# The first head's probabilities of an eight-head attention turned by VectorE through DRAM, and its weighed sum put behind the second head's gate

## The chip, the cores and the metric

The kernel runs on one core of one Trainium2 chip. The metric is the device time of one execution in microseconds (us); the median of three runs stands for the kernel. Engines are named as the profile names them: PE is TensorE's matmul, PEld its weight load, DVE is VectorE, ACT is ScalarE, POOL is GpSimd, SP is SyncE, which here only issues DMAs.

## The reference

One block of a hybrid model on 512 tokens and 16 meta tokens (528 rows): a feed-forward stage, a retention, an attention over chosen keys, and a second feed-forward stage. The change touches the attention: eight heads of 128, with rotary positions, a softmax over the admitted keys, the weighed sum of the values, and beside it the gates, sigmoids of further projections of the same input `u`.

```python
aq = rope(aq.reshape(B, T, ATT_HEADS, ATT_DH), pos)
ak = rope(ak.reshape(B, T, ATT_HEADS, ATT_DH), pos)
...
ya = dsa_attention(aq, ak, av, iq, ik, iw, k_top).reshape(B, T, ATT_W) @ w_att_out
merged = jax.nn.sigmoid(g_ret) * yr + jax.nn.sigmoid(g_att) * ya
...
# in dsa_attention, per head:
s = jnp.einsum(q, k) * scale          # masked to the admitted keys
p = jax.nn.softmax(s)
out = p[..., :N_META] @ v_meta + p[..., N_META:] @ v_sel
```

(The lines behind the comment are shortened: the reference gathers the chosen keys, the kernel masks the others with a bias.)

## The kernel before

All products are of fp32 accuracy: each operand is split into a high and a low half in a rounded format, and each product is the sum of three matmuls (high by high, high by low, low by high). A split is one copy on ACT (the high half) and one subtraction on DVE (the low half); both are recorded at lines 117 and 118, in `split`.

A projection (queries, keys or a gate) is 8 steps of three matmuls on a weight of 1024 by 128. The weight comes by a DMA on SP's queue into one of two `raw` buffers (L133) and is split into one of three pairs of buffers, `whi` and `wlo`. So a weight's DMA can only be issued once the low half of the weight two before it is subtracted, and a weight's split can only begin once PE has ended the projection three before it.

In the attention stage PE does, head after head: the scores of head h (15 matmuls, `score`), the queries of head h+1 (`psaq`, 24), the keys of head h+1 (`psak`, 48 of 264 columns), the weighed sum of head h-1 (`psao`, 12 and a tail for the meta keys), and a gate (`psgate` or `psga`, 24). Softmax and the rotary step run on DVE, ACT and POOL behind it. The order on each engine is the order in which a scheduler of the language put the instructions when the kernel was built; it holds at run time: each engine, and each queue, takes its instructions in that order and waits where one isn't ready. Tile numbers such as `whi_9979` are the program's own.

The weighed sum wants the probabilities with keys on the partitions, so they are transposed. In the kernel before there are two ways. Heads 1 to 7: `turn` transposes 32 by 32 blocks on DVE into `cross` (L2084), four POOL DMAs write that to DRAM (`pd`, L2088), `turned` reads it back in ten SP DMAs into `land0` to `land3` (L2096, L2100, L2103), one for each 128 keys, and `turned_parts` splits each piece into `pth` and `ptl`. Head 0: `transpose_p` does 14 transposes on PE (L2132, L2134) into PSUM, and the pieces are split from there.

The values of heads 0 to 3 and of heads 4 to 7 are split in two steps, the second behind the sums of the first head and partly behind the scores of the second (`late_v`).

Of the kernel before, what the change touches and what calls it, by code (L numbers as in the profile page):

```python
# [18 lines left out]
P = 128  # L19
# [62 lines left out]
def kernel(ctx: ExitStack, tc: tile.TileContext, x, meta, g1, wg1, wu1, wd1, gm,  # L82
# [77 lines left out]
    class Cols:  # L160


        def __init__(self, src, c0, n, nk=KD, step=2):
            self.src, self.c0, self.n, self.nk, self.step = src, c0, n, nk, step
            self.at, self.raw = 0, None
# [4 lines left out]

        def next(self):
            return split_w(self.next_raw())
# [1258 lines left out]
    def split_values(raw, parts, apart=False):  # L1431
# [5 lines left out]
        late = lambda: nc.vector.tensor_tensor(lo, src, hi.bitcast(F32), ALU.subtract)  # L1437
        if apart:
            return late, split_values_of(parts)
        late()  # L1440
# [557 lines left out]
    with pool("ao") as ao:  # L1998
        vo = [ao.tile([P, AH, S], F32R, tag=f"vo{i}", name="vo") for i in range(2)]
        ao_parts = [(vo[0][:, c, :], vo[1][:, c, :]) for c in range(AH)]  # L2000
        with pool("at") as at:
# [21 lines left out]
            def proj_q(w=None):  # L2023
                w = w or cq.next()
# [10 lines left out]
            def proj_k():  # L2035
                w = ck.next()
                parts, ps = halves(mm_tile("psak"))
                mm3(parts, w, xs, KD)
                return rope_k(ps)

            def rope_k(ps, eng=nc.gpsimd):
# [37 lines left out]

            def turn(h):  # L2080
# [46 lines left out]
            def transpose_p():  # L2127
                parts = []
                for kb in range(4):
                    ps = sm_tile("psPT")  # L2130
                    for j in range(max(kb - 1, 0), 4):
                        nc.tensor.transpose(ps[:, j * P : (j + 1) * P], prob[j][:, kb * P : (kb + 1) * P], ident)  # L2132
                    if kb == 3:
                        nc.tensor.transpose(ps[:NM, 0:P], prob[3][:, 4 * P : T], ident)  # L2134
                    n = S - KQ[kb]
                    ph, pl = part_tiles(kb, n)
                    if kb == 3:
                        split_rows(ps[:NM, P - NM : P], tp["p"][:, :NM], "hlh")
                    split(ps[:, KQ[kb] :], ph, pl)
                    parts.append((ph, pl))  # L2140
                return parts
# [873 lines left out]
```

## Time and profile before

| what | number |
|---|---|
| runs | 1474.12, 1473.36, 1473.56 us; median 1473.56 |
| the profiled execution | 1473.46 us, of which the span of the instructions is 1471.7 us |
| PE busy | 1463.0 us, 99% of the span |
| DVE, ACT, POOL busy | 1136.4 us (77%), 737.1 us (50%), 252.7 us (17%) |
| chain that ended last | 95% of it on PE |

Times in rows are microseconds from the start of the span; 1.8 us of the profiled execution lie outside it. The attention stage that the change touches runs from about 877 to 1070 us. "x13" in a row says that it stands for 13 instructions, and an arrow gives out<-in.

### The profile page before, as it was taken

The numbers are of one execution on the slowest core, as the hardware profiler recorded it, in microseconds if no ns is written. First come the engines' busy times: TensorE is split into PE (matmuls) and PEld (weight loads), VectorE is DVE, ScalarE is ACT, GpSimd is POOL, SyncE is SP. The second block draws the span as 40 slices with busy tenths as digits, with TensorE's granted clock in tenths as the row PEclk, the third lists the DMA queues.
The fourth block names the chain that finished last, engine by engine and source line by source line (L and its number), as shares of the span: only waits on it lengthen the run. The fifth ranks groups of instructions, "written<-read, shape, count | busy, mean of one in ns | idle before, by whom it ended". The sixth has DMA issues, their size and how long they took to land.

```text
span 1471.7 us, 22839 instructions
## 1 busy us (share of the span) xinstructions
PE 1463.0 (99%) x8773; PEld 1299.4 (88%) x8773; DVE 1136.4 (77%) x1761; ACT 737.1 (50%) x1065; POOL 252.7 (17%) x354
## 2 busy tenths in 40 slices
PE   9999999999999999999999999999999999999998
PEld 8999999999988888989898888899888888888886
DVE  5997586686786876687979788778567788888887
ACT  6655264364354445443333428667534645555454
POOL 2001010012311113111111142332101301101100
PEclk9999999999999999999999999999999999999999
DMA  5266476567957839476767664676847347757652
GB/s 176 74 179 177 140 189 166 149 164 209 302 138 246 257 94 310 118 207 161 198 167 194 157 157 114 162 183 172 224 157 257 123 164 268 248 186 271 216 192 94
DMA packets 215502, 270.74 MB, mean 184 GB/s; under 512 B 38368, under 2 KB 137464, under 8 KB 214752
## 3 DMA queue, kind: packets, MB, share of 16 engines
q1 hardware_dynamic: 187104, 204.30, 43.7%
q0 software_dynamic: 25616, 60.23, 18.2%
q10 hardware_dynamic: 2672, 4.74, 1.0%
q8 instruction: 69, 1.13, 0.3%
q14 instruction: 41, 0.34, 0.1%
HBM read 238.01 MB, written 81.54 MB: 217 GB/s over the span
## 4 chain that ended last, share of the span: by engine, by line
PE 95%; DVE 2%; ACT 1%; issue 1%; DMA 0%; POOL 0%; DVEq 0%; ACTq 0%
PE psd L157 9%; PE psqX L157 7%; PE psqX L2539 7%; PE psrg L157 6%; PE psro L157 6%; PE psd L2512 5%; PE psvX L1249 4%; PE psqY L2539 4%; PE psqY L157 4%; PE psrk L157 3%; PE psrq L157 3%; PE psga L157 3%; PE psat L157 3%; PE psmo L157 3%; PE psak L157 3%; PE psaq L157 3%
## 5 line engine op out<-in xcount | busy, mean ns | idle before, releaser
L378 ACT ACTIVATE whi<-raw 128x1024 fp32r<-128x1024 f32 (+2 forms) x165 | 157.3, 956 | 116.9 <-PE psd L157 32.9
L379 DVE TENSOR_TENSOR wlo<-raw,whi 128x1024 fp32r<-128x1024 f32 (+2 forms) x165 | 185.2, 1125 | 22.7 <-ACT whi L378 22.6
L378 ACT ACTIVATE whi<-w 128x1024 fp32r<-128x1024 f32 x58 | 61.3, 1058 | 58.0 <-PE psd L2512 17.2
L379 DVE TENSOR_TENSOR wlo<-w,whi 128x1024 fp32r<-128x1024 f32 x58 | 70.3, 1216 | 22.4 <-ACT whi L378 22.3
L157 PE MATMUL psro<-vo,whi 128*128 128x512 f32 x256 | 78.9, 389 | 0.0
L157 PE MATMUL psd<-hl,whi 128*128 128x264 f32 x352 | 71.4, 284 | 0.0
L157 PE MATMUL psd<-hh,wlo 128*128 128x264 f32 x352 | 70.8, 283 | 0.0
L157 PE MATMUL psd<-hh,whi 128*128 128x264 f32 x352 | 70.6, 282 | 0.0
L118 DVE TENSOR_TENSOR wlo<-raw,whi 128x1024 fp32r<-128x1024 f32 (+1 forms) x43 | 53.9, 1254 | 14.1 <-ACT whi L117 13.8
L157 PE MATMUL psqX<-th,whi 128*128 128x264 f32 x216 | 61.1, 283 | 0.0
L157 PE MATMUL psqX<-tl,whi 128*128 128x264 f32 x216 | 61.1, 283 | 0.0
L157 PE MATMUL psqX<-th,wlo 128*128 128x264 f32 x216 | 61.1, 283 | 0.0
L2418 POOL DMA_DIRECT2D hts<-cross x36 | 23.3, 652 | 208.2 <-DVE cross L2414 207.9
L117 ACT ACTIVATE whi<-raw 128x1024 fp32r<-128x1024 f32 (+1 forms) x43 | 44.2, 1034 | 27.1 <-PE psga L157 10.9
L157 PEld LDWEIGHTS psro<-vo,whi 128*128 128x128 f32 x256 | 48.0, 188 | 10.1
L157 PEld LDWEIGHTS psd<-hh,wlo 128*128 128x128 f32 x352 | 54.5, 188 | 0.0
L157 PEld LDWEIGHTS psd<-hh,whi 128*128 128x128 f32 x352 | 54.2, 188 | 0.0
L157 PEld LDWEIGHTS psd<-hl,whi 128*128 128x128 f32 x352 | 53.8, 188 | 0.0
L378 ACT ACTIVATE whi<-wsum 128x1024 fp32r<-128x1024 f32 x36 | 38.1, 1059 | 30.4 <-PE psd L157 14.8
L157 PE MATMUL psrg<-xh,whi 128*128 128x512 f32 x128 | 50.5, 395 | 0.0
L157 PE MATMUL psrg<-xl,whi 128*128 128x512 f32 x128 | 49.9, 390 | 0.0
L157 PE MATMUL psrg<-xh,wlo 128*128 128x512 f32 x128 | 49.9, 390 | 0.0
(640 smaller groups left out, 4812.0 us busy)
## 6 DMA issues: line engine op xcount, KB each, us to landing
raw<-in_w_in_dram SPq DMA_DIRECT2D x18, 1024.0 KB, 5.9
raw<-in_w_in_dram SPq DMA_DIRECT2D x33, 512.0 KB, 4.2
w<-in_w_in_dram SPq DMA_DIRECT2D x24, 512.0 KB, 6.9
raw<-in_ffn_w_up_dram SPq DMA_DIRECT2D x11, 1024.0 KB, 5.8
raw<-in_ffn_w_gate_dram SPq DMA_DIRECT2D x10, 1024.0 KB, 5.4
w<-in_ffn_w_gate_dram SPq DMA_DIRECT2D x20, 512.0 KB, 4.7
raw<-in_ffn_w_down_dram SPq DMA_DIRECT2D x18, 512.0 KB, 6.9
raw<-in_ffn_w_down_dram SPq DMA_DIRECT2D x12, 768.0 KB, 4.9
```

The source lines that it names most:

```text
L117: nc.scalar.activation(hi, src, AF.Copy)
L118: eng.tensor_tensor(lo, src, hi.bitcast(F32), ALU.subtract)
L157: nc.tensor.matmul(o, a[:, k, :], b[:, sl], start=first and k == 0 and i == 0, stop=last and k == nk - 1 and i == 2, skip_group_check=onto)
L378: nc.scalar.activation(hi, src, AF.Copy)
L379: return lambda: nc.vector.tensor_tensor(lo, src, hi.bitcast(F32), ALU.subtract)
L1249: nc.tensor.matmul(d[bank_][t], a, b[:, k, :], start=not onto and j + k + m == 0, stop=j + k == 3 and m == 2, skip_group_check=onto)
L2418: by.dma_start(d.rearrange("(b i) a e -> a i b e", i=32)[a], cross[32 * a : 32 * a + 32].rearrange("p b c t -> p b (c t)"))
L2512: nc.tensor.matmul(ps[:, t], a, b[:, k, :], start=not onto and k + m == 0, stop=k == 1 and m == 2, skip_group_check=onto)
L2539: nc.tensor.matmul(ps[:, t], a, b[:, k, :], start=not onto and j + k + m == 0, stop=j + k == 3 and m == 2, skip_group_check=onto)
```

## The change

It turns head 0's probabilities as those of the other heads are: `turn(0)` stands behind head 1's keys, `turned(0)` behind that, and the 14 transposes on PE and `transpose_p` are gone. The weighed sum of head 0 goes behind the gate of that iteration instead of ahead of it. To make room and time: `cross` exists from the stage's start, in the bytes that later hold the low halves of the second four heads' values; these values are split at h == 2; the rotary product of head 1's keys is done by DVE instead of POOL; the key weight of head 1 is taken between the first head's scores and the gate's weight right behind them (`ahead`); and the small DMA of the meta keys' block goes from `turn` to `turned`.

```diff
+        def ahead(self):
+            self.held = split_w(self.next_raw())
+            self.at -= 1
...
-        vo = [ao.tile([P, AH, S], F32R, tag=f"vo{i}", name="vo") for i in range(2)]
-        ao_parts = [(vo[0][:, c, :], vo[1][:, c, :]) for c in range(AH)]
+        vo = [ao.tile([P, n, S], F32R, tag=f"vo{i}", name="vo") for i, n in enumerate((AH, 4))]
+        cross = ao.tile([P, 16, 4, 32], F32, tag="vo2", name="cross")
+        ao_parts = [(vo[0][:, c, :], vo[1][:, c, :]) for c in range(4)]
...
-            def proj_k():
-                w = ck.next()
+            def proj_k(w, eng=nc.gpsimd):
...
-                nc.gpsimd.dma_start(land[4], crosst[96 : 96 + NM, NM:])
-
-            def turned(h):
+            def turned(h):
+                nc.gpsimd.dma_start(land[4], crosst[96 : 96 + NM, NM:])
...
-                for to_one in [score(j, q, k) for j in (2, 1, 0, 3)]:
+                to_ones = [score(2, q, k)]
+                wk = ck.next()
+                for to_one in to_ones + [score(j, q, k) for j in (1, 0, 3)]:
                     to_one()
-                vs = split_values(raw, [v[:, :4, :] for v in vo])
-                raw = fetch_values(5, vraw())
+                gr.ahead()
             pend = None
             for h in range(AH):
                 more = h + 1 < AH
                 if h == 1:
                     with tc.manual_schedule(engines=BUSY):
-                        to_ones = [score(j, q, k) for j in (2, 1, 0, 3)]
-                        late_v()
-                        for to_one in to_ones:
+                        for to_one in [score(j, q, k) for j in (2, 1, 0, 3)]:
                             to_one()
+                        turn(1)
+                        pend = turned_parts()
                 elif h:
                     scores(q, k)
                 if more:
-                    q, k = proj_q(w if h == 0 else None), proj_k()
+                    if h:
+                        q, k = proj_q(cq.next()), proj_k(ck.next())
+                    else:
+                        q = proj_q(w)
+                        with tc.manual_schedule(engines=BUSY):
+                            k = proj_k(wk, nc.vector)
+                            turn(0)
+                            vs = split_values(raw, [v[:, :4, :] for v in vo])
+                        turned(0)
+                        raw = fetch_values(5, vraw())
...
+                if h == 1:
+                    wide_gate(sm_tile("psga"))
                 if pend is not None:
-                    (weigh_turned, weigh_v)[h == 1](h - 1, pend, vs[h - 1])
-                if h == 0:
-                    with tc.manual_schedule(engines=BUSY):
-                        late_v, more_v = split_values(raw, [v[:, 4:, :] for v in vo], True)
-                        vs += more_v
-                if h == 1:
+                    weigh_turned(h - 1, pend, vs[h - 1])
+                if h == 2:
...
-                    if more:
-                        turn(h)
-                    wide_gate(sm_tile("psga"))
+                    if h > 1:
+                        if more:
+                            turn(h)
+                        wide_gate(sm_tile("psga"))
                     turned(h)
```

How the built order differs is seen at two places. The first is around head 0's weighed sum, whose pieces come on SP's queue and are split on ACT. On SP's queue the first read of a turned head in the kernel before is head 1's:

```order
L133 DMA raw_9983<-in_w_in_dram 128x8x128
L133 DMA raw_10076<-in_w_in_dram 128x8x128
L133 DMA raw_10185<-in_w_in_dram 128x8x128
L2096 DMA land0_9320<-pd_88 128x512
L2100 DMA land1_9321<-pd_88 128x32
```

After the change the first one is head 0's, and these rows end with its last read (`raw_9977` is the weight of the fourth head's keys, `raw_10082` that of the gate behind head 1's sum, `raw_10192` that of the fifth head's queries):

```order
L133 DMA raw_9977<-in_w_in_dram 128x8x128
L133 DMA raw_10082<-in_w_in_dram 128x8x128
L133 DMA raw_10192<-in_w_in_dram 128x8x128
L2107 DMA land0_9321<-pd_88 128x512
L2111 DMA land1_9322<-pd_88 128x32
L2114 DMA land1_9322<-pd_88 128x4x32 x3
L2111 DMA land2_9323<-pd_88 128x32
L2114 DMA land2_9323<-pd_88 128x4x32 x2
L2111 DMA land3_9324<-pd_88 128x32
L2114 DMA land3_9324<-pd_88 128x4x32
```

So head 0's ten reads stand behind the issue of `raw_10192`. On ACT, after the change, head 0's four pieces (`pth_9679` to `pth_9691`) stand like this (`psak_9747` are the third head's keys, `psgate_9814` is the gate now ahead of the sum):

```order
L117 ACTIVATE whi_9979<-raw_9977 128x1024
L1378 ACTIVATE tmp_9797<-psak_9747 64x528
L1379 ACTIVATE tmp_9797<-psak_9747 64x528
L117 ACTIVATE aq_9737<-tmp_9730 128x512
L117 ACTIVATE whi_10084<-raw_10082 128x1024
L117 ACTIVATE pth_9679<-land0_9321 128x512
L117 ACTIVATE ak_9803<-tmp_9796 128x528
L1476 ACT_TABLE_LOAD
L1476 ACTIVATE gate_9839<-psgate_9814 128x512
L117 ACTIVATE pth_9683<-land1_9322 128x416
L117 ACTIVATE pth_9687<-land2_9323 128x288
L117 ACTIVATE pth_9691<-land3_9324 128x160
```

The first piece stands behind the split of a weight two further on, the other three behind the gate's sigmoid. The second place is DVE around head 1's pieces (the low halves `ptl`), while head 2 is being turned into `cross`. In the kernel before:

```order
L2084 STREAM_TRANSPOSE cross_9816<-pj0_9312 128x5x32
L118 TENSOR_TENSOR ptl_9880<-land1_9321,pth_9879 128x416
L2069 TENSOR_SCALAR pj3_9318<-pj3_9318,stat_9935 128x528
L118 TENSOR_TENSOR wlo_10188<-raw_10185,whi_10187 128x1024
L118 TENSOR_TENSOR ptl_9884<-land2_9322,pth_9883 128x288
L1372 TENSOR_TENSOR tmp_9972<-psaq_9947,cos_9306 128x512
L118 TENSOR_TENSOR ptl_9888<-land3_9323,pth_9887 128x160
```

After the change:

```order
L1380 TENSOR_TENSOR tmp_9966<-psaq_9941,cos_9307 128x512
L2096 STREAM_TRANSPOSE cross_10068<-pj2_9317 128x13x32
L118 TENSOR_TENSOR ptl_9870<-land0_9321,pth_9869 128x512
L1382 TENSOR_TENSOR tmp_9966<-tmp_9966,tmp_9967 128x512
L2096 STREAM_TRANSPOSE cross_10068<-pj1_9315 128x9x32
L2096 STREAM_TRANSPOSE cross_10068<-pj0_9313 128x5x32
L118 TENSOR_TENSOR ptl_9874<-land1_9322,pth_9873 128x416
L118 TENSOR_TENSOR aq_9974<-tmp_9966,aq_9973 128x512
L2096 STREAM_TRANSPOSE cross_10068<-pj3_9319 128x16x32
L2097 STREAM_TRANSPOSE crosst_9326<-pj3_9319 128x32
L118 TENSOR_TENSOR wlo_10195<-raw_10192,whi_10194 128x1024
L118 TENSOR_TENSOR ptl_9878<-land2_9323,pth_9877 128x288
```

All of head 1's low halves, four transposes and a weight's low half now stand behind the rotary product of the fourth head's queries (`psaq_9941`), which in the kernel before came behind the third piece.

## Rows read from the trace of the kernel before

**Rows 1.** The page: busy time of the engines, share of the span, instructions.

```profile
PE 1463.0 (99%) x8773; PEld 1299.4 (88%) x8773; DVE 1136.4 (77%) x1761; ACT 737.1 (50%) x1065; POOL 252.7 (17%) x354
```

**Rows 2.** Waits of PE: us in total, times, longest.

```profile
PE psaq L157 <- DVE ptl L118: 0.3, 1, 0.3
```

**Rows 3.** Windows: length; busy PE, PEld, DVE, ACT, POOL; PEclk, DMA share, GB/s.

```profile
877.00:945.00 68.00, 67.72 (x395) 59.73 (x394) 55.20 (x120) 48.12 (x83) 19.31 (x30) 1.00 0.49 134
945.00:1070.00 125.00, 125.00 (x697) 110.09 (x696) 88.33 (x208) 80.77 (x147) 32.26 (x43) 1.00 0.73 194
```

**Rows 4.** Timeline of PE at head 0's transposes: start, duration, engine, line, operation.

```profile
901.70 1.58 PE L2132 MATMUL psPT<-ident,pj 128*128 128x128 f32 x13
903.12 0.27 PE L2134 MATMUL psPT<-ident,pj 128*16 128x128 f32 x1
903.15 0.48 PE L157 MATMUL psgate<-xh,whi 128*128 128x512 f32 x1
```

**Rows 5.** Timeline of PE at head 1's scores.

```profile
908.73 2.15 PE L2058 MATMUL psS<-ak,aq 128*128 128x400 f32 x15
```

**Rows 6.** Timeline of DVE ahead of head 1's scores.

```profile
906.07 1.22 DVE L118 TENSOR_TENSOR vo<-vraw,vo 128x1024 fp32r<-128x1024 f32 x1
907.21 0.70 DVE L118 TENSOR_TENSOR ak<-tmp,ak 128x528 fp32r<-128x528 f32 x1
```

**Rows 7.** The chain that ended last, 900 to 960: start, duration, engine, tile.

```profile
916.88 5.77 PE psak L157 x48
922.65 1.90 PE psao L1624 x12
...
924.61 5.59 PE psgate L157 x24
...
943.44 1.96 PE psao L2123 x12
```

**Rows 8.** Timeline of ACT, 929 to 936.

```profile
930.01 1.06 ACT L117 ACTIVATE whi<-raw 128x1024 fp32r<-128x1024 f32 x1 [1.40 <-PE psgate L157]
931.09 1.28 ACT L1471 ACT_TABLE_LOAD   x1
932.39 0.60 ACT L1471 ACTIVATE gate<-psgate 128x512 f32<-128x512 f32 x1
...
934.93 0.20 ACT L1454 ACTIVATE ptail<-land 16x16 fp32r<-16x16 f32 x1
```

**Rows 9.** The tile land: duration in ns (min/median/max), first and last start, forms.

```profile
L117 ACT ACTIVATE pth<-land x28: 321/490/634, 935.9 to 1067.5; 128x512 fp32r<-128x512 f32 x7, 128x416 fp32r<-128x416 f32 x7, 128x288 fp32r<-128x288 f32 x7, 128x160 fp32r<-128x160 f32 x7
L118 DVE TENSOR_TENSOR ptl<-land,pth x28: 310/571/1684, 936.6 to 1067.9; 128x512 fp32r<-128x512 f32 x7, 128x416 fp32r<-128x416 f32 x7, 128x288 fp32r<-128x288 f32 x7, 128x160 fp32r<-128x160 f32 x7
```

**Rows 10.** Timeline of SP's queue: the first and the last read of head 1.

```profile
930.70 0.34 SPq L2096 DMA_DIRECT2D land<-pd  x1
...
936.10 0.52 SPq L2103 DMA_DIRECT2D land<-pd  x1
```

**Rows 11.** DMA issues, 880 to 960: count, KB each, median us to landing.

```profile
land<-pd SPq DMA_DIRECT2D x11, 64.0 KB, 2.6
land<-pd SPq DMA_DIRECT2D x2, 256.0 KB, 3.4
```

**Rows 12.** The tile cross: DVE's transposes.

```profile
L2084 DVE STREAM_TRANSPOSE cross<-pj x28: 302/546/714, 916.5 to 1047.7; 128x416 f32<-128x416 f32 x7, 128x288 f32<-128x288 f32 x7, 128x160 f32<-128x160 f32 x7, 128x512 f32<-128x512 f32 x7
```

**Rows 13.** The tile psao: DVE's subtraction of 512 columns.

```profile
L118 DVE TENSOR_TENSOR vo<-psao,vo x8: 676/684/693, 927.9 to 1069.7; 128x512 fp32r<-128x512 f32 x8
```

**Rows 14.** Timeline of DVE around head 2's last piece, 950 to 968.

```profile
965.38 0.32 DVE L118 TENSOR_TENSOR ptl<-land,pth 128x160 fp32r<-128x160 f32 x1
965.95 1.22 DVE L118 TENSOR_TENSOR wlo<-raw,whi 128x1024 fp32r<-128x1024 f32 x1 [0.25 <-ACT whi L117]
```

**Rows 15.** Windows behind the last matmul (columns as in rows 3).

```profile
1465.70:1467.00 1.30, 0.00 (x0) 0.00 (x0) 1.18 (x3) 1.17 (x4) 0.00 (x0) 1.00 0.56 217
...
1468.00:1469.00 1.00, 0.00 (x0) 0.00 (x0) 0.00 (x0) 0.00 (x0) 0.00 (x0) 0.50 0.83 327
```

More of the change, by code (lines that the diff above doesn't have):

```diff
@@ L164, in __init__ @@
             self.src, self.c0, self.n, self.nk, self.step = src, c0, n, nk, step
[L165 removed]
+            self.at, self.raw, self.held = 0, None, None
         def next_at(self, i):
             self.at = i
+        def ahead(self):
+            self.held = split_w(self.next_raw())
+            self.at -= 1
         def next(self):
[L172 removed]
+            if self.held is None:
+                return split_w(self.next_raw())
+            w, self.held = self.held, None
+            self.at += 1
+            return w
         def next_raw(self):
@@ L1429, in tails, with split_values @@
         tp.update(v=stacked(p, "vtail", S), p=stacked(p, "ptail", n))
-    def split_values(raw, parts, apart=False):
+    def split_values(raw, parts):
         src, (hi, lo) = raw[:, 2:4], (p[:, 2:4, :] for p in parts)
@@ L1436, in split_values @@
         nc.scalar.activation(hi, src, AF.Copy)
[L1437 to L1440, printed above, removed]
+        nc.vector.tensor_tensor(lo, src, hi.bitcast(F32), ALU.subtract)
         return split_values_of(parts)
@@ L2078, in part_tiles, with empty @@
                 return [at.tile([P, S - Q0[kb]], F32R, tag=f"pt{c}{kb}", name=f"pt{c}")[:, :n] for c in "hl"]
+            def empty(t):
+                for j in range(3):
+                    nc.gpsimd.memset(t[:, 4 * j + 5 :, j, :], 0.0)
+                return t
+            empty(cross)
             def turn(h):
@@ L2125, in weigh_turned @@
                 split(ps, *ao_parts[h])
[L2127 to L2141, printed above, removed]
-            def weigh_v(h, parts, v):
-                ps = mm_tile("psao")[:, :S]
-                weighted(ps, v, parts)
-                split(ps, *ao_parts[h])
             def wide_gate(tile=None):
@@ L2190 @@
                         turn(h)
+                if h == 1:
+                    wide_gate(sm_tile("psga"))
                 if pend is not None:
-                    (weigh_turned, weigh_v)[h == 1](h - 1, pend, vs[h - 1])
-                if h == 0:
-                    with tc.manual_schedule(engines=BUSY):
-                        late_v, more_v = split_values(raw, [v[:, 4:, :] for v in vo], True)
-                        vs += more_v
-                if h == 1:
+                    weigh_turned(h - 1, pend, vs[h - 1])
+                if h == 2:
+                    for r in (0, 2):
+                        nc.scalar.activation(vo[0][:, 4 + r : 6 + r, :], raw[:, r : r + 2], AF.Copy)
+                    vo.append(ao.tile([P, 4, S], F32R, tag="vo2", name="vo"))
+                    more_v = [vo[0][:, 4:, :], vo[2]]
+                    for r in (0, 2):
+                        hi, lo = (p[:, r : r + 2, :] for p in more_v)
+                        nc.vector.tensor_tensor(lo, raw[:, r : r + 2], hi.bitcast(F32), ALU.subtract)
+                    vs += split_values_of(more_v)
+                    ao_parts += [(more_v[0][:, c, :], more_v[1][:, c, :]) for c in range(4)]
                     vrs.close()
                     crp = crs.enter_context(pool("cross", 1, side="right"))
-                    cross = crp.tile([P, 16, 4, 32], F32, tag="cross", name="cross")
-                    for j in range(3):
-                        nc.gpsimd.memset(cross[:, 4 * j + 5 :, j, :], 0.0)
+                    cross = empty(crp.tile([P, 16, 4, 32], F32, tag="cross", name="cross"))
                 if h:
-                    if more:
-                        turn(h)
-                    wide_gate(sm_tile("psga"))
+                    if h > 1:
+                        if more:
+                            turn(h)
+                        wide_gate(sm_tile("psga"))
                     turned(h)
```

8 lines of the change are left out of this document (3 added, 5 removed).

## The prediction

> **What bounds the kernel now.** I read the page first: PE is busy in 99% of the span [rows 1], so a wait of PE costs its own length, and work taken from another engine gains nothing by itself. Then the windows of the stretch that the change touches: 67.72 busy of 68.00 us up to 945, and 125.00 of 125.00 after it, at a granted clock of 1.00 [rows 3]. Then PE's waits, to see what the missing 0.28 is: one wait of the third head's queries for a low half of head 0's probabilities, whose PSUM bank they take [rows 2]. The reader is to see that this stage has nearly no wait to give back. The change can gain by taking matmuls away, and it loses wherever a piece now comes late. So I walked each weighed sum with the new order of the instructions and the durations of the rows. All times are of one profiled execution of 1473.46 us, 0.1 below the median of the three runs; its span is 1471.7, and the sum is made against 1473.46.
>
> **What is saved.** The 14 transposes on PE start at 901.70 and the gate behind them at 903.15 [rows 4]: 1.45 us from start to start, 0.104 each. The wait of 0.28 [rows 2] goes, since that PSUM tile is gone. Head 0's sum, in the wider form of the other heads, takes 1.96 instead of 1.90 [rows 7]. Together -1.67.
>
> The last transpose's own duration is 0.27 [rows 4], but they overlap, and the step from start to start is what PE pays. The Trainium skill, "TensorE: Matmul & The Clock Gate", Part 4: PE-mode transpose, gives about 275 ns for one such transpose inside a kernel. By that, 14 would be worth 3.85 us, and the whole forecast would be 2.4 lower, 1478.8. The row agrees with the 275 ns as a duration, and not as a price in a run of them, so 1.45 stands.
>
> **Wait B: head 1's scores for their keys.** Before, the low half of these keys ends at 907.21 + 0.70 = 907.91 and the scores start at 908.73 [rows 6, 5]: 0.82 to spare. PE now comes 1.45 earlier. If the keys are ready when they were, the scores wait 0.4, as the low half is wanted one product in (2.15 for 15, [rows 5], so 0.14), and 1.45 - 0.82 - 0.14 leaves some 0.4 to 0.5. On DVE a subtraction of values (1.22, [rows 6]) goes out of the way and a weight's low half of the same size comes in, with the rotary product (about 0.7, as a DVE row of 528 columns, [rows 6]). The lower bound is 0, if the removal of all three subtractions ahead of it outweighs that; the upper is 1.6, if one 1.22 is added to the 0.4. I take 0.6, nearer to the case in which things stay.
>
> **Wait C: head 0's sum.** Let E be the end of the third head's key products; before it is 916.88 + 5.77 = 922.65 [rows 7]. Then comes the gate, 5.59, and then the sum, 1.96 [rows 7], which would end at E+7.5 with no wait. Two chains come later than that.
>
> The first is that of SP's queue. The fourth head's key weight takes the third one's buffer, so its high half starts at E; 1.06 on ACT [rows 8], 1.22 on DVE for its low half [rows 6], E+2.3. Only that frees the buffer into which `raw_10192` goes, and the ten reads of head 0 stand behind that issue. With 0.6 for handing on and for issuing the weight the first read goes out at E+2.9. Ten reads take from 930.70 to 936.10 in the row [rows 10], so the last goes out at E+8.3. A read of 64 KB lands in 2.6 (the first, 256 KB, in 3.4) [rows 11]: E+10.9. Then a copy of 0.32 and a subtraction of 0.31, the least of their rows [rows 9], and the last product and the tail, 0.3: the sum ends at E+11.8. That is 4.3 of waiting.
>
> The second is ACT's order. `whi_10084` waits for the end of the gate, as its like before waited 1.40 for one [rows 8]; behind it come the first piece, the keys' high half, the table load, the sigmoid and three pieces. From the gate's end: 1.06 + 0.62 + 0.65 + 1.28 + 0.60 with 0.62 as the middle of the wide pieces of 0.49 to 0.63 and 0.65 as an estimate for 528 columns from the same [rows 8, 9], then 0.54 + 0.45 + 0.32 for the pieces (sum of three within 0.32 to 0.63, [rows 9]) and 0.6 for the last subtraction and product: 6.1, against 2.0 for a sum that doesn't wait. That is 4.1; where the first piece is not yet there or the keys' high half waits for DVE, up to 0.9 more. I take 4.6. Lower bound 3, if reads issue and land faster than in the row; upper 6, if DVE's order adds one more subtraction of 1.22 in front.
>
> What is queued behind: head 2's scores wait on PE itself, the fourth head's queries behind them. POOL has time.
>
> **Wait D: head 1's sum, third piece.** Let Q be the end of the fourth head's query products. Behind Q ACT does a weight's high half 1.06, two meta pieces of 0.2 and two rotary halves of 0.6 as the gate's row [rows 8]: 2.66. Then DVE has, in the new order, the cosine product 0.68, four transposes at 0.546 [rows 12] = 2.18, a narrow one of under 0.2, three low halves of pieces at 0.57 [rows 9] = 1.71, the sum of the rotary step and the queries' low half at 0.68 each [rows 13], and a weight's low half 1.22: 7.3. So the third piece is there at Q+10.0. PE comes to that product after the keys (5.77, [rows 7]) and some two thirds of the sum (1.4): Q+7.2. A wait of 2.8; a DVE instruction starts a little before the one ahead is recorded as ended (906.07 + 1.22 = 907.29 against 907.21, [rows 6]), so I take 2.7, with 1 (half of DVE's rows done before the cosine product's turn) and 3.3 (one more low half of 0.57 ahead) as the bounds. In the kernel before, the same pieces stood ahead of the cosine product and nothing waited.
>
> **Wait E: head 2's sum, last piece.** Before, this low half ends at 965.38 + 0.32 = 965.70, and right behind it comes a weight's low half, 965.95 to 967.17 [rows 14]. PE's need was at about 966.0 (the sum of head 2 starts 20.8 behind that at 943.44, by the step of the two sums in [rows 7], and the last piece is 1.75 into it), so 0.3 was to spare. In the new order the weight's halves stand ahead of that piece: it is ready at 967.17 + 0.32 = 967.5, a wait of 1.5. Bounds 0.5 and 2. From head 3 on, the order around the sums is that of before, and PE runs with no wait again; nothing in that stretch gives time back, as PE had none to give [rows 3].
>
> The rest of the edits costs nothing: the values' second split lies behind heads 2's softmax, on engines busy for 65 to 71% there [rows 3]; the moved DMA of 1 KB stands on POOL, which is 26% busy.
>
> **Sum.** -1.67 + 0.6 + 4.6 + 2.7 + 1.5 = +7.7: 1473.46 + 7.7 = **1481.2**. Its own range is 1478.5 to 1483.5. A measurement of this kernel tells 0.2%, 2.9 us, from no change.
>
> **Rivals.**
> 1. Only B and C are paid. After C, PE is 4.6 later, and DVE and ACT have used that time to come ahead; head 1's and head 2's pieces are then in time. For it: both waits are sums of many short steps with a spread. Against: the late pieces are late against query products of the same head, which are pushed back as well. -1.67 + 0.6 + 4.6 = +3.5: 1477.0.
> 2. Not slower: the reads of head 0 land in time. If the first read goes out about 4.3 earlier than E+2.9, that is ahead of the weight's issue, and the pieces stand ahead of the sigmoid, C is gone, and with C the late start of D and E. For it: the probabilities themselves are in DRAM long before. Against: SP's and ACT's orders. At most -1.67: 1471.8. As that is 0.11%, faster by over 0.2% has hardly a way.
> 3. PE's clock falls in C. In a stretch of 1.30 us with no matmul the granted clock was still 1.00, and a microsecond behind that stretch it was 0.50, 1.2 GHz [rows 15]. If the waits of C brought it down for the scores that follow (2.15, [rows 5]), these would take twice as long: +2.2, 1483.4. Against: products stand between the pieces of C, so no single idle time is as long as that. The Trainium skill, "TensorE: Matmul & The Clock Gate", Part 1, says that the gate has these two levels and follows PE's activity; the rows agree, and no row of this stage shows it below 1.00.
>
> **How the numbers follow.** The forecast 0.55, only B and C 0.20, not slower 0.08, the clock 0.10, and 0.07 for anything else. The range is 1475.5 to 1485.0: the low end takes in nearly all of rival 1 and the sum of the low bounds (-1.67 + 0 + 3 + 1 + 0.5 = +2.8, 1476.3), the high end rival 3 and the sum of the high ones (-1.67 + 1.6 + 6 + 3.3 + 2 = +11.2, 1484.7). Slower by over 0.2% (above 1476.4) has the forecast, the clock, over half of rival 1 and most of the rest: 0.82. Within 0.2% has the other part of rival 1 and rival 2: 0.16. Faster: 0.02.
>
> **What would show it.** In PE's waits after the change: no row with psPT; head 1's scores on their keys for 0.6; head 0's sum on its pieces for 4 to 5 in all, in three or four parts; head 1's on one low half for 2.7; head 2's on one for 1.5; none in heads 3 to 7. SP's timeline shows the first read of head 0 right behind a weight's issue. The prediction is wrong if that read goes out before E, if the gate's end doesn't hold the first piece's copy back, or if the trace shows PE busy through 920 to 950.

## The result, and the profile after

The changed kernel takes 1489.17 us (median of five runs, 1486.99 to 1490.16) against 1473.93 for the kernel before on the same chips: ratio 1.0102, interval 1.0088 to 1.0117, 15.2 us slower. The forecast was slower by 7.7, so the sign and the places were right, and the size was half of the measured one; 1489 lies above the range. The profiled execution took 1490.1, 0.9 above the median, with a span of 1488.3.

PE's waits, on the page's terms the first thing to read (us in total, times, longest):

```profile
PE psao L2134 <- ACT pth L117: 5.2, 3, 3.0
PE psao L2134 <- DVE ptl L118: 4.0, 4, 1.5
...
PE psS L2062 <- DVE ak L118: 0.2, 1, 0.2
```

The wait of the third head's queries [rows 2] is gone, the sums of heads 0 to 2 wait, head 1's scores wait 0.2. These rows make 9.4 us; the loss is 15.2 in the medians and 16.6 in this execution. The windows show what is missing (columns as in rows 3; PEclk is the third number from the end):

```profile
900.00:925.00 25.00, 24.75 (x144) 21.69 (x144) 20.63 (x41) 18.28 (x27) 7.70 (x9) 1.00 0.68 189
925.00:950.00 25.00, 18.88 (x90) 14.95 (x89) 17.01 (x42) 14.01 (x28) 6.16 (x8) 0.80 0.62 141
950.00:975.00 25.00, 23.54 (x132) 20.45 (x131) 20.04 (x46) 15.22 (x28) 6.78 (x12) 0.93 0.57 148
975.00:1000.00 25.00, 23.30 (x130) 20.44 (x129) 17.70 (x42) 14.98 (x28) 5.41 (x7) 0.93 0.57 144
1000.00:1070.00 70.00, 70.00 (x393) 61.93 (x393) 52.60 (x127) 48.67 (x86) 20.73 (x28) 1.00 0.72 189
```

Up to 925 and from 1000 on PE is as full as before [rows 3]. Between, it idles 9.3 us in three windows, and in all three the granted clock is below 1.00. Finer windows of the same kernel:

```profile
926.00:928.00 2.00, 0.25 (x2) 0.00 (x0) 2.00 (x7) 1.58 (x2) 0.00 (x0) 1.00 1.09 338
928.00:930.00 2.00, 0.69 (x1) 0.19 (x1) 2.00 (x3) 1.38 (x3) 1.83 (x3) 0.85 0.98 174
930.00:932.00 2.00, 1.05 (x2) 0.50 (x2) 1.51 (x3) 1.99 (x3) 0.98 (x3) 0.50 1.07 200
...
938.00:940.00 2.00, 2.00 (x11) 1.99 (x10) 0.71 (x3) 1.88 (x2) 0.36 (x1) 0.59 0.62 116
940.00:942.00 2.00, 2.00 (x14) 1.78 (x14) 2.00 (x12) 1.36 (x5) 0.00 (x0) 1.00 0.47 73
...
954.00:956.00 2.00, 0.73 (x7) 0.73 (x7) 2.00 (x5) 0.81 (x2) 0.76 (x2) 1.00 0.01 2
956.00:958.00 2.00, 2.00 (x8) 1.64 (x8) 2.00 (x2) 0.60 (x1) 2.00 (x3) 0.68 0.93 204
958.00:960.00 2.00, 2.00 (x6) 1.52 (x5) 1.57 (x3) 0.39 (x1) 1.63 (x3) 0.50 1.03 333
```

In head 0's sum the clock goes to 0.50 (1.2 GHz) while PE mostly waits, and is back only when head 2's scores are nearly done. At head 1's sum PE does 0.73 in 954 to 956 at 1.00, and it is the gate behind the wait that runs at 0.50, with PE busy all the time. The DMA engines are full here: shares of 1.09, 0.98 and 1.07. Single windows of 2 us reach that in the kernel before too (1.09 in 948 to 950); what is new is that it lasts. In windows of 5 us, first after the change, then before it:

```profile
925.00:930.00 5.00, 1.94 (x7) 0.90 (x5) 5.00 (x9) 2.96 (x5) 2.45 (x4) 0.94 0.95 229
930.00:935.00 5.00, 3.00 (x5) 1.29 (x5) 2.83 (x4) 2.17 (x3) 2.07 (x3) 0.50 1.03 235
```

```profile
925.00:930.00 5.00, 5.00 (x23) 4.13 (x22) 4.00 (x5) 2.01 (x3) 2.99 (x4) 1.00 0.49 115
930.00:935.00 5.00, 5.00 (x29) 4.44 (x29) 3.24 (x13) 4.93 (x7) 1.29 (x1) 1.00 0.80 198
```

The starts of PE's groups in the two timelines, and the difference, tell where each microsecond went:

| start of | before | after | later by |
|---|---|---|---|
| gate behind the second head's keys | 903.15 | 901.37 | -1.78 |
| third head's keys | 916.72 | 914.84 | -1.88 |
| their end, E | 922.49 | 920.61 | -1.88 |
| third head's scores (behind gate and head 0's sum) | 930.04 | 937.91 | +7.87 |
| fourth head's queries | 932.03 | 940.77 | +8.74 |
| head 1's sum | 943.27 | 952.01 | +8.74 |
| gate behind it | 945.30 | 956.00 | +10.70 |
| next scores | 950.84 | 963.18 | +12.34 |
| head 2's sum | 964.08 | 976.42 | +12.34 |
| gate behind it | 966.11 | 980.65 | +14.54 |
| next scores | 971.66 | 987.78 | +16.12 |
| last head's sum | 1066.92 | 1082.88 | +15.96 |

So head 0's sum lost 9.75, the scores behind it 0.87 (slow), head 1's sum 1.96, the gate behind it 1.64 (slow), head 2's sum 2.20, the gate behind it 1.58 (slow); heads 3 to 6 nothing. The last sum lost another 0.8.

How head 0's sum came to end so late stands in the chain that ended last (start, duration, what), read from the wait backwards:

```profile
911.46 8.47 DMA vraw<-vst
...
919.95 1.91 ACT vo L2197 x2
...
921.90 1.07 ACT whi L117
...
922.99 1.24 DVE wlo L118
...
924.25 0.37 SPq L133
...
924.79 0.45 SPq L2107
...
928.40 0.52 SPq L2114
...
928.97 6.50 DMA land<-pd
...
935.57 0.45 ACT pth L117
...
936.06 1.90 PE psao L2134 x6
```

It is the predicted chain, weight's high half, low half, the queue, the reads, the piece, with two transfers in it that are much longer than thought: the load of values (1 MB) took 8.47 (5.0 in the kernel before), so the first read left at E+4.2 instead of E+2.9; and a read of the third piece took 6.5 instead of 2.6 [rows 11]. Beside it, the writes of head 1's turn went out at 928.17 to 930.81 on POOL.

### The profile page after: what moved, and what is told of

It is laid out like the page before. It is cut to its first block, busy times and chain, and to the rows that moved or that the text cites. A ratio compares the mean times of both kernels' runs of the same rounds, so it can differ in the third digit from the quotient of the medians.

```text
span 1488.3 us, 22860 instructions
## 1 busy us (share of the span) xinstructions
PE 1469.8 (99%) x8759; PEld 1301.5 (87%) x8759; DVE 1139.1 (77%) x1767; ACT 737.4 (50%) x1065; POOL 257.0 (17%) x361
## 5 line engine op out<-in xcount | busy, mean ns | idle before, releaser
L157 PEld LDWEIGHTS psro<-vo,whi 128*128 128x128 f32 x256 | 48.0, 188 | 10.2
```

Of the source, the lines that this page charges most:

```text
L157: nc.tensor.matmul(o, a[:, k, :], b[:, sl], start=first and k == 0 and i == 0, stop=last and k == nk - 1 and i == 2, skip_group_check=onto)
```

## The experiments

Every ratio is to the kernel before on the same chip. "Loses" is what a group takes beyond its time in the kernel before, its waits and slow matmuls taken together, in the profiled execution.

**1. Fillers in the waits.** Matmuls that nobody reads keep PE busy while it waits.

```diff
+            FILL = {0: {(0, 0): 13, (0, 1): 6, (1, 0): 2, (1, 1): 5, (2, 0): 8}, 1: {(2, 1): 6}, 2: {(3, 0): 3, (3, 1): 4}}
...
+                        for _ in range(FILL.get(h, {}).get((kb, i), 0)):
+                            nc.tensor.matmul(both[:, S:], vh, xs(0)[0][:, REAL], start=True, stop=True)
```

> The changed kernel, with matmuls that nobody reads put into the waits of the first three weighed sums: 13, 6, 2, 5 and 8 of 512 columns (0.23 us each) ahead of five products of head 0's sum, 6 ahead of one of head 1's, 3 and 4 ahead of two of head 2's. They write into the second, unused bank of the sum's own PSUM tile, so the result is the same. Theory A (each long wait lets PE's clock fall, and the slow matmuls behind it cost as much as a wait): the granted clock stays at 1.00 through 925 to 990, the scores behind head 0's sum take 2.0 instead of 2.86, the gates behind head 1's and head 2's sums 5.55 instead of 7.2 and 7.1, some products of head 0's sum 1.1 less: about 5 us less than the changed kernel, 1484. Theory B (the waits alone make the 15 us, the clock is a side effect that is hidden in them): the same time as the changed kernel, 1487 to 1490, or more by what the fillers overrun.

1484.86 us, ratio 1.0072 (1.0055 to 1.0089): 4.3 less than the changed kernel, for work added.

```profile
925.00:950.00 25.00, 24.52 (x127) 20.22 (x126) 20.13 (x48) 15.19 (x31) 7.55 (x11) 1.00 0.65 154
950.00:975.00 25.00, 25.00 (x153) 22.57 (x152) 19.78 (x45) 14.93 (x27) 7.54 (x10) 1.00 0.62 163
```

The clock stays at 1.00, the scores behind head 0's sum take 2.1, the gates 5.55. The sums still end as late (11.6 behind the gate for head 0, 11.8 in the changed kernel). The clock's part is shown: some 4 of the 15, as the three slow groups behind the sums make in the table above (0.87, 1.64 and 1.58).

**2. Reads of head 0 early on SP's queue; the queue in written order for two iterations.**

```diff
+                    sp.enter_context(tc.manual_schedule(engines={mybir.EngineType.SP}))
...
+                if h in (1, 2):
+                    if h == 2:
+                        ga.ahead()
+                    rq = cq.next_raw()
+                    turned(h - 1)
+                    pend = turned_parts()
...
```

The split of the pieces is written behind the reads with them.

> The changed kernel, with SP's queue in written order for the second and third iteration, so that head 0's ten reads stand ahead of the weight of the fourth head's keys instead of behind the two weights after it; head 1's reads come behind the weights as before. Theory A (head 0's sum waits for reads that leave late and land slowly because they meet the writes of the next head): the first read leaves at about 916 instead of 924.8, the pieces have landed before the gate ends, and head 0's sum waits some 2.5 for ACT's and DVE's order alone, instead of 9.8 from the gate's end; with one fall of the clock less the total is 1479 to 1483. Theory B (the place of the pieces on ACT, behind a weight that waits for the gate's end and behind the sigmoid, sets the wait wherever the reads land): the sum ends still 4 to 6 later than without a wait, and the total stays above 1484.

1488.56 us, ratio 1.0102 (1.0087 to 1.0117). The first read leaves at 920.38, and head 0's sum ends 3.4 earlier behind the gate, with 6.4 of loss instead of 9.8. That is close to theory B (4 to 6, above 1484): DVE's order holds the pieces now. And head 1's sum loses 5.9 instead of 2.0; nothing is left in the total. PE's rows of the two sums:

```profile
928.95 0.50 PE L2135 MATMUL psao<-ptl,vo 128*128 128x512 f32 x1 [1.44 <-DVE ptl L118]
...
932.36 0.72 PE L2135 MATMUL psao<-ptl,vo 128*128 128x416 f32 x1 [1.76 <-DVE ptl L118]
...
955.36 0.61 PE L2135 MATMUL psao<-ptl,vo 128*128 128x288 f32 x1 [3.54 <-DVE ptl L118]
```

**3. Only the gate ahead of the sum, in the kernel before.**

```diff
+                if h == 1:
+                    wide_gate(sm_tile("psga"))
                 if pend is not None:
...
-                    wide_gate(sm_tile("psga"))
+                    if h > 1:
+                        wide_gate(sm_tile("psga"))
```

> The kernel before with one edit: the second head's gate ahead of the first head's weighed sum. The transposes on PE, the values and the rotary product stay as they were. If the order of gate and sum by itself breaks the order on ACT and DVE for the sums of heads 1 and 2 (theory B2), there are waits of 1 to 2 us at these sums, and 1476 to 1480. If only the way through DRAM makes pieces late (theory A), no wait but at most 0.4 us, 1473.5 to 1474.5.

1474.68 us, ratio 1.0007 (0.9997 to 1.0016). The order of gate and sum costs nothing that can be told.

**4. Head 1's turn late,** behind head 0's sum.

```diff
-                        turn(1)
                         pend = turned_parts()
...
+                    if more:
+                        turn(h)
                     if h > 1:
-                        if more:
-                            turn(h)
                         wide_gate(sm_tile("psga"))
```

> The changed kernel with head 1's turn (five transposes on DVE, four writes of 256 KB to DRAM) behind head 0's weighed sum, where those of the later heads stand, instead of ahead of the third head's queries. Theory A's part on the landing (the last reads of head 0 took 6.5 us because they met these writes): the third and fourth pieces land 2.6 to 3.5 after their issue, head 0's sum waits 3 less, and head 1's reads come later instead, so that head 1's sum waits for them: 1486 to 1490 in total, but with the wait moved from head 0's sum to head 1's. Theory C (the weights on the same queue, not the writes, slow the reads): landing stays at 6 us and head 0's sum as it is.

1493.83 us, ratio 1.0130 (1.0113 to 1.0146): worse than expected. Head 0's third piece came 2.1 earlier (its copy started at 933.44), which is the part of head 1's turn in the 6.5; but head 1's sum lost 4.4 and head 2's 4.1.

**5. Head 0 on PE again, the rest of the change kept** (`transpose_p` and `weigh_v` are the functions of the kernel before).

```diff
-                        pend = turned_parts()
...
-                            turn(0)
...
-                        turned(0)
...
-                    weigh_turned(h - 1, pend, vs[h - 1])
+                    (weigh_turned, weigh_v)[h == 1](h - 1, pend, vs[h - 1])
...
                 else:
+                    pend = transpose_p()
                     wide_gate()
```

> The changed kernel with head 0's probabilities transposed on PE again as in the kernel before, so head 0 has neither the turn on DVE nor writes nor reads; everything else of the change stays (the gate ahead of the sum, the values split at the third head, the rotary product of the second head's keys on DVE, the weights taken early). Theory A (the way of head 0 through DRAM makes the waits): no wait at the weighed sums, the clock stays up, and at most a wait of 3 at the third head's scores for their keys, which the order of ACT and DVE now puts late: 1473.5 to 1477.5. Theory D (the other edits, by the order that they give to ACT and DVE, make the sums of heads 1 and 2 late on their own): waits of 1.5 to 2 with a slow gate behind each at these two sums, 1480 to 1484.

1481.85 us, ratio 1.0050 (1.0035 to 1.0065). The time is theory D's, but no sum waits; the place is the one that theory A named, with waits of 3.8 and 0.9 instead of at most 3, and slow matmuls behind them: 7 us are lost there.

```profile
PE psS L2062 <- ACT ak L117: 3.8, 1, 3.8
...
PE psS L2062 <- DVE ak L118: 1.1, 2, 0.9
```

The third head's scores wait for their keys, and run slow behind the wait. On ACT and POOL:

```profile
928.59 1.06 ACT L117 ACTIVATE whi<-raw 128x1024 fp32r<-128x1024 f32 x1 [4.54 <-DMA raw<-in_w_in_dram]
...
932.45 0.64 ACT L117 ACTIVATE ak<-tmp 128x528 fp32r<-128x528 f32 x1
```

```profile
919.58 2.60 POOL L2100 DMA_DIRECT2D pd<-cross  x4 [6.67 <-issue]
922.20 1.31 POOL L1381 TENSOR_TENSOR tmp<-tmp,sin 128x512 f32<-128x512 f32 x1
...
924.12 1.66 POOL L1381 TENSOR_TENSOR tmp<-tmp,sin 128x528 f32<-128x528 f32 x1 [0.62 <-ACT tmp L1379]
```

The four writes of head 1's turn stand in one piece ahead of the rotary products, and the keys (`ak`) stand on ACT behind a weight that lands late: ACT waits 4.54 for it. The second of these orders is what counts, and DVE has it too: its sum of the rotary step comes at 930.82, behind the low half of that weight. POOL's product for the keys had ended at 925.78.

**6. Reads early as in experiment 2, and head 0's sum behind the fourth head's queries.**

```diff
-                        q, k = proj_q(cq.next()), proj_k(ck.next())
+                        q = proj_q(split_w(rq) if rq is not None else cq.next())
+                        if h == 2:
+                            weigh_turned(0, pend, vs[0])
+                        k, rq = proj_k(ck.next()), None
...
-                if pend is not None:
+                if pend is not None and h > 1:
```

> The kernel with the early reads (e2_reads_early) and head 0's weighed sum behind the fourth head's queries instead of behind the second head's gate. Theory A: by then all pieces of head 0 have long come, so there is no wait at its sum; what is late instead are the third head's keys for the scores right behind the gate (2 to 3), and head 1's pieces (4 to 6, as in e2_reads_early): 1480 to 1486. If the order on DVE holds head 0's pieces back wherever the sum stands, its wait of 6 stays and the total is above 1488.

1488.81 us, ratio 1.0095 (1.0078 to 1.0112); the profiled execution was the slowest of its runs (1493.52), so only its order of events is used: head 0's sum had no wait, and the third head's keys and head 1's pieces were late in its place. The total missed the expected range.

**7 and 8. No reads of head 0; no reads of head 1.** The sum goes over what the tiles hold, in experiment 7 and 9 zeros that POOL wrote once.

```diff
             def turned(h):
                 nc.gpsimd.dma_start(land[4], crosst[96 : 96 + NM, NM:])
+                if h == 0:
+                    return
```

In experiment 8 it is `if h == 1`, in 9 `if h < 2`.

> The changed kernel without head 0's ten reads: its pieces are split from a buffer of zeros, so this head's output is left out, and the time is that of the kernel without these transfers. Theory A: the wait at head 0's sum loses what the reads make of it, 3 to 5 of 9.8, and what is left (1 to 3) is the order on DVE, and 2 to 3 of wait at the third head's scores for their keys; heads 1 and 2 keep their waits: 1483 to 1487. Theory B (order on ACT and DVE alone): the sum of head 0 ends as late as before, 1488 to 1490.

> The changed kernel without head 1's ten reads: its pieces are split again from what head 0 left, so this head's output is left out, and the order on ACT and DVE is one in which they don't wait for a transfer. Head 0's sum keeps its 9.8. If head 2's wait follows from head 1's lateness (theory E1), both waits and both slow gates go: 2.0 + 1.6 + 2.2 + 1.6 = 7.4 less than the changed kernel, 1481.8. If head 2's wait has its own cause in the order of its last piece (theory E2), only head 1's part goes: 1485.5.

Without head 0's reads 1490.77 us, ratio 1.0110 (1.0095 to 1.0125), above both theories: head 0's sum loses 0.8 instead of 9.8, but the scores behind it, which wait for their keys, now lose 4.7, and the sums of heads 1 and 2 lose 5.1 and 5.0. Without head 1's reads 1484.35, ratio 1.0067 (1.0052 to 1.0082): head 2's sum takes 2.02 and the gate behind it 5.54, no wait at all. The waits and slow gates of both heads go, as theory E1 says (the total falls by 4.8 instead of its 7.4). So head 2's wait doesn't stand by itself; it comes with head 1's reads.

**9. No reads of either.**

> The changed kernel without the ten reads of head 0 and without those of head 1 (zeros are split and weighed, both heads' outputs are left out). Theory A2 (a late chain: whatever is taken from head 0's sum comes back at the next thing that is late, the third head's keys, and at head 2's sum): waits of 3 to 6 at the third head's scores, some at head 2's sum, 1481 to 1486. Theory A (the reads of both heads make the time): 1473 to 1477.

1486.99 us, ratio 1.0089 (1.0074 to 1.0104). Head 0's sum loses 1.9, the third head's scores 3.8 (3.0 of it waits for their keys), the queries behind them 1.3, head 2's sum 5.9 and the gate behind it 1.1: what was taken from the first place came back at the next. That is theory A2, 1 us above its range.

**10. Values' first split and the load of the others back to their old place.**

```diff
                 gr.ahead()
+                vs = split_values(raw, [v[:, :4, :] for v in vo])
+                raw = fetch_values(5, vraw())
...
                             turn(0)
-                            vs = split_values(raw, [v[:, :4, :] for v in vo])
                         turned(0)
-                        raw = fetch_values(5, vraw())
```

> The changed kernel with the first four heads' values split, and the load of the others' (1 MB) issued, ahead of the second head's queries as in the kernel before, so this load no longer runs beside the writes of head 0 and ahead of the weight of the fourth head's keys. Theory G (the load of 1 MB, which took 8.5 us, holds back the copies of values on ACT, the weight behind them, and with it the reads of head 0): the first read leaves 1.3 earlier after the third head's keys than 4.2, head 0's sum waits 1.3 to 3 less, and the second head's scores wait up to 1 more for their keys: 1485.5 to 1488. Otherwise the time of the changed kernel, 1487 to 1490.

1487.77 us, ratio 1.0097 (1.0082 to 1.0113). The first read left at 924.28, E+2.9, the predicted time; head 0's sum lost 8.1 instead of 9.8. In the total it can't be told from the changed kernel. One thing in this run speaks against a simple rule for the clock. Head 1's sum has the same wait of 1.46, with PE's busy time nearly that of the changed kernel in 954 to 956, and yet the gate behind it runs at full clock (5.55):

```profile
954.00:956.00 2.00, 0.83 (x7) 0.83 (x8) 2.00 (x5) 0.72 (x2) 0.86 (x2) 1.00 0.07 6
956.00:958.00 2.00, 2.00 (x11) 1.66 (x10) 2.00 (x1) 0.60 (x1) 2.00 (x3) 1.00 0.92 237
958.00:960.00 2.00, 2.00 (x10) 1.65 (x10) 1.48 (x3) 0.49 (x1) 1.53 (x3) 1.00 0.96 311
```

**11. Head 0 on PE, and head 1's turn late:** the diffs of experiments 4 and 5 together.

> The changed kernel with head 0's transposes on PE again (e5_pe_again) and head 1's turn, with its four writes, behind head 0's weighed sum, where the kernel before has it, instead of ahead of the third head's queries. e5_pe_again lost 7 us at the third head's scores, which waited for their keys. Theory F (the place of head 1's turn makes these keys late: its four writes go out on POOL in one piece ahead of the rotary products, and ACT's order then has a weight that comes late ahead of the keys): the waits go but for 0.5 to 1, 1473.5 to 1476. Theory G (the load on the DMA engines, by the values' load that now falls into this stretch, makes the weight and so the keys late): the wait stays at 3 or more, 1478 to 1482.

1474.30 us, ratio 1.0007 (0.9997 to 1.0016): as fast as the kernel before. Against experiment 5 only the place of head 1's turn differs in the program, and with it some 7 us go (7.5 between the medians, 6.9 when each is taken against the kernel before). The built order differs by more than the turn. On ACT the keys now stand ahead of the late weight:

```profile
928.36 0.64 ACT L117 ACTIVATE ak<-tmp 128x528 fp32r<-128x528 f32 x1 [2.19 <-DVE tmp L1382]
928.91 1.04 ACT L117 ACTIVATE whi<-raw 128x1024 fp32r<-128x1024 f32 x1
```

On POOL a write, the rotary product of the queries and a write alternate again, but the product of the keys comes no earlier; it ends at 926.61, against 925.78 in experiment 5:

```profile
925.29 1.32 POOL L1381 TENSOR_TENSOR tmp<-tmp,sin 128x528 f32<-128x528 f32 x1 [3.10 <-ACT tmp L1379]
```

So of theory F the order on ACT is borne out, and the four writes ahead of the rotary products are not what made the keys late.

**12. Head 0's sum ahead of the gate again,** the rest as changed.

```diff
-                if h == 1:
-                    wide_gate(sm_tile("psga"))
                 if pend is not None:
                     weigh_turned(h - 1, pend, vs[h - 1])
+                if h == 1:
+                    wide_gate(sm_tile("psga"))
```

> The changed kernel with head 0's weighed sum ahead of the second head's gate, as in the kernel before; head 0 still goes through DRAM. If the gate ahead of the sum covers its own length of the wait (theory A), the sum ends about where it did, some 17 behind the third head's keys, and the gate comes behind it, slow: 5.5 to 7 more, and 1.5 to 3.6 less at the sums of heads 1 and 2 for which PE then comes later: 1490 to 1494. If the supply on ACT, DVE and the queue sets the pace whatever PE does in the meantime (theory A2), the later waits shrink by as much as the first grows: 1487 to 1490.

1488.93 us, ratio 1.0115 (1.0093 to 1.0137). That is theory A2: head 0's sum now loses 14.6 instead of 9.8, the slow group behind it 1.4, and the sums of heads 1 and 2 nothing. The gate ahead of the sum is worth nothing here.

**13 to 15. What head 0's turn costs when nobody needs it.** Into the kernel of experiment 11 comes `turn(0)` alone, then `turned(0)` too, while PE still turns head 0's probabilities itself; and the kernel of experiment 7 gets head 1's turn late (the diff of experiment 4).

```diff
                             k = proj_k(wk, nc.vector)
+                            turn(0)
                             vs = split_values(raw, [v[:, :4, :] for v in vo])
+                        turned(0)
```

> The kernel with PE's transposes for head 0 and head 1's turn late (e15_pe_turn1, 1474.3), with head 0's five transposes on DVE and its four writes of 256 KB added; nobody reads what they write. Theory H (head 0's turn costs by itself, through DVE's time and the DMA engines, before any piece is read): the second head's softmax or the third head's keys come late, waits of 4 to 6 with a slow stretch, 1479 to 1482. Theory I (only the reads and the pieces of head 0 cost): 1474 to 1476.

> The same with head 0's ten reads too, into the buffers that head 1's reads use next; head 0's sum still takes PE's transposes. Theory H: 2 to 5 more than e20_turn0_write, as the reads stand ahead of head 1's on the queue and head 1's sum waits: 1481 to 1487. Theory I: 1477 to 1481 against 1474 to 1476 for e20_turn0_write.

> The changed kernel without head 0's ten reads (zeros are split and weighed, this head's output is left out) and with head 1's turn behind head 0's sum. If two causes are each enough (the reads of head 0, the early turn of head 1), taking both away gives 1475 to 1479. If head 0's turn alone already makes head 1 late (theory H), head 1's sum waits 5 to 7 with slow matmuls behind it, 1484 to 1490.

1481.70 us (ratio 1.0052, 1.0037 to 1.0067), 1484.53 (1.0075, 1.0058 to 1.0092) and 1488.65 (1.0098, 1.0083 to 1.0113). The turn on DVE and its writes cost 7.4 with no reader, the reads 2.8 more. The loss of the first is in several small waits at a clock of 1.00: 1.3 of the third head's queries for DVE, 2.3 of the third head's scores for keys, 1.1 of head 1's sum, 0.6 of head 2's. All three totals lie where theory H puts them. DVE had been full there already; of 5 us, in experiment 11 and then in 13 (the third pair of numbers is DVE):

```profile
910.00:915.00 5.00, 5.00 (x26) 4.23 (x26) 4.97 (x12) 4.44 (x8) 1.30 (x1) 1.00 0.83 272
```

```profile
910.00:915.00 5.00, 3.73 (x21) 3.06 (x20) 4.94 (x9) 3.40 (x5) 3.70 (x5) 1.00 0.73 138
```

PE goes from 5.00 to 3.73 where DVE has no room for the turn.

## Why the prediction was too low

In the profiled execution the loss is 16.6, where 7.7 were forecast. Of the 8.9 between them 5.1 are the size of wait C, the slow matmuls inside it counted in, and 4.1 are slow matmuls behind the three sums, for which the sum had no term; the other differences nearly cancel.

- **What is saved** (-1.67): right. From the second head's keys to the gate the gain grew from 0.33 to 1.78, so the 14 transposes were worth 1.45; at E it was 1.88.
- **Wait B** (+0.6): 0.25.
- **Wait C** (+4.6): the place and both chains were right, the size was not: 9.75, above the bound of 6. Two durations were taken from a quieter stretch. The step "a read of 64 KB lands in 2.6" measured 6.5 for the third piece, and the load of values, which the change moves into this stretch, 8.47; experiments 4 and 10 give 2.1 and some 1.7 back by taking head 1's writes and this load away; the rest of the 5.1 has no run of its own. I had counted head 0's reads, and not the two moves that put a megabyte each into the same microseconds.
- **The rivals, clock** (+2.2 in one place, chance 0.10): the granted clock fell three times, and filling the waits gave 4.3 back (experiment 1). "No single idle time is as long as that" (1.30) was wrong for C, where PE waited 3.0 in one piece; and it was asked of C alone, although the forecast had single waits of 2.7 and 1.5 at D and E. So the premise that a wait of PE costs its own length is a step that failed: at head 1's sum 1.46 of waiting were followed by a gate 1.64 longer. It doesn't fail each time: behind the same wait in experiment 10 the gate lost nothing, and what decides it no run here shows.
- **Waits D and E** (+2.7, +1.5): 1.96 and 2.20. In D it was the predicted piece that waited (PE 955.27, 1.46 for DVE). In E it was the last piece, as forecast. But that this is a wait of its own, by the order of that piece, is not borne out: in experiments 2, 8 and 12 the same sum ran without a wait.
- **"The rest of the edits costs nothing":** for what that sentence names it held, as experiment 11 keeps all of the change but head 0's way through DRAM and the place of head 1's turn, and takes 1474.30. What it left out failed in kind. Head 1's turn ahead of the third head's queries costs some 7, by the order that ACT and DVE get with it (experiment 5 against 11), and head 0's turn 7.4 before any piece of it is read (experiment 13 against 11). I had costed neither at the place where it displaces other work, only the waits for their pieces.

The theory that I held after the result, that late reads make the wait, fell too: head 0's reads early (experiment 2), without them (7) and without those of both heads (9), the total stayed within 2.2 us; only without head 1's alone (8) was it 4.8 less. What the runs show is a stretch in which DVE, ACT's order and the DMA engines together are late, and PE waits at whichever sum or scores come first; only experiment 11, with head 0's turn taken out and head 1's back in its old place, gives all of the time back. How the 15 us split between the two turns stays open: alone they cost some 7 and 7.4 (10.2 with the reads), together 15, but with head 1's turn late and head 0's left in, the time is 1488 to 1494 (1493.83 in experiment 4; 1488.65 in 15, without head 0's reads), so they are not independent. No version was faster than the kernel before.

## What to carry to other kernels

Where PE is 99% busy, moving 1.5 us of its work to an engine that is full in just those microseconds lost here; the moved work alone cost 7.4 before anyone read its result: read the busy share of the receiving engine in windows of 5 us at that place, not over the stage. Price a transfer with the load that it will meet after the change, its own new traffic included. A step that is moved in the program also changes the built order of other engines, so read those orders again around it. When a wait is removed and the time does not move, look for the next late input before trusting the first theory; an experiment that takes the whole work out tells more than one that makes it earlier.

## What the runs showed of the hardware

In the changed kernel the granted clock fell behind a wait of PE of 1.46 us, and not in the wait but after it: 0.50 in 958 to 960 with PE busy for all of it, while 954 to 956, with the wait, had 1.00. In head 0's longer wait it fell while PE still waited (0.50 in 930 to 932). Behind the same 1.46 us in experiment 10 it stayed at 1.00, so the length of a wait alone doesn't tell.

Two-input operations of DVE and POOL slow each other. The same subtraction of 1024 columns on DVE, alone and beside a product on POOL, in the changed kernel, and the product:

```profile
904.14 1.22 DVE L118 TENSOR_TENSOR wlo<-raw,whi 128x1024 fp32r<-128x1024 f32 x1
...
911.84 2.18 DVE L118 TENSOR_TENSOR wlo<-raw,whi 128x1024 fp32r<-128x1024 f32 x1
```

```profile
912.82 2.35 POOL L1480 TENSOR_TENSOR accr<-accr,gate 128x512 f32<-128x512 f32 x1
```

A product of this shape takes 1.31 on POOL in experiment 5, at 922.20, beside this subtraction on DVE:

```profile
922.84 1.76 DVE L118 TENSOR_TENSOR wlo<-raw,whi 128x1024 fp32r<-128x1024 f32 x1 [1.37 <-ACT whi L117]
```

There POOL starts first and keeps its time, and DVE ends 1.09 behind POOL's end. The Trainium skill, "SBUF — State Buffer", SBUF: two separate sides, says that the two engines share a pair of ports under an exclusive lock that is held for a whole instruction. The pair of experiment 5 agrees with it: 1.09 behind POOL's end is nearly the whole subtraction. In the pair of the changed kernel POOL ends 1.15 behind DVE's end, which fits; why DVE, which starts first by the rows, takes 2.18, the rows do not show. Writes that POOL only issues did not lengthen DVE's rows: the subtraction at 929.08 takes 1.21 while POOL issues four of them from 928.17 to 930.81. This was not tried in an experiment of its own.
